# The opening of a diffusion backbone step: first modulation's weights in ring buffers, six units ahead on the first half of h, idle matmuls on TensorE

## The chip, the cores and the metric

The kernel runs on one core of one Trainium2 chip. The metric is the time of one execution on the device in microseconds (us). Before the change it is 2283.66 us, the median of 3 runs (2283.55 to 2283.94).

## What is computed

One inference step of a two-layer backbone on 512 latent tokens and 128 context tokens of width 1024, all in float32. Each layer is a half-step SwiGLU FFN, a token mixer (a Fourier mixer in layer 0, attention in layer 1) and another half-step FFN. Each sub-layer stands in a norm whose shift, scale and gate come from the conditioning vectors. Only the opening of layer 0 matters here:

```python
def _modulation(cond, w_mod, b_mod):
    m = jax.nn.silu(cond) @ w_mod + b_mod
    return m.reshape(cond.shape[0], N_MOD, D_MODEL)

def _modulated_prenorm(x, g, m, k):
    return _rmsnorm(x, g) * (1 + m[:, 3 * k + 1, None]) + m[:, 3 * k, None]

def _half_ffn(x, m, k, g_pre, g_post, w1, w2):
    h = _modulated_prenorm(x, g_pre, m, k)
    return x + 0.5 * m[:, 3 * k + 2, None] * _rmsnorm(_swiglu(h, w1, w2), g_post)
```

So the first FFN can't multiply by `w1` before the first two of the nine modulation vectors (shift and scale) are there, each a product of the conditions with 1024 x 1024 weights.

## The kernel before

Activations lie transposed: 8 chunks of 128 channels on the partitions, the 640 tokens as columns in two halves of 320. A float32 product is made of three fast ones: each operand is split into a rounded part `hi` (ScalarE, L215) and the rest `lo` (VectorE, L216), and `mm3` (L228 to L230) multiplies hi x hi, hi x lo and lo x hi. In the profile's names of a product, `main<-ring,hi`, the first input is h and the second the weights.

A *unit* is one 128 x 1024 block of weights: a 512 KB load into one of 4 `raw` buffers (L157) and a split into a `hi` and a `lo` buffer (6 of each, the pool `wts`), or, for a few units, into two blocks of the ring of 20 (`ring`, 128 x 1280). Units 0 and 1 are gate and up of the FFN's column 0, units 2 and 3 of column 1, 4 and 5 of column 2, 6 and 7 (in ring blocks) of column 3. One unit times one half of h is 8 chunks x 3 = 24 products.

`begin` (L299) opens the kernel:

- x of the first half is loaded. `first` (L383) squares and sums it, TensorE adds over the channels (L502), GpSimd takes the power (L507), TensorE spreads the result over the partitions (L512), and VectorE scales x into `y` (L391).
- The weights of shift and scale come as 16 loads of 512 KB (`first`, L320) in two parts of 8. Part 0 gives the coefficients of chunks 0 to 3, part 1 those of chunks 4 to 7. They take `hi` and `lo` buffers of the pool of units. Each tile is multiplied by four small matmuls (128x256, 32 rows of output, L323) as it lands.
- `coefs` (L333): ScalarE reads the sums (L330), TensorE turns them (L346), and VectorE makes the coefficients in four small operations (L339, L434 to L438). Then the four chunks get scale and shift, by VectorE for even (L400) and by ScalarE for odd ones (L398), and are split.
- `products` (L353) multiplies chunks 0 to 3 by units 0 and 1, then comes part 1 of the weights, then chunks 0 to 3 by units 2 and 3. What is left, chunks 4 to 7 of these four units, is kept in `begun` and run by `ffn` (L602) as its first step. Units 4 to 7 and the other half of h follow there. The norm of the other half (`launch`, `pre`) is woven between, with its L502 and L512 on TensorE and its L538, L544 and L546 on VectorE and ScalarE.

All loads but two of x go through SyncE's queue in the order of the program. Every engine works through its own list in order; a scheduler settles that order when the program is built, with marked stretches (`high_priority`) ahead and `behind_of` holding an instruction behind others. So a row that waits holds all rows after it on its engine.

Of the kernel before, what the change touches and what calls it, by code (L numbers as in the profile page):

```python
# [18 lines left out]
P = 128  # L19
# [91 lines left out]
class Kernel:  # L111
    def __init__(self, ctx, tc, io, subs=6):
        self.tc, self.nc, self.io, self.subs = tc, tc.nc, io, subs
        pool = lambda name, bufs, **k: ctx.enter_context(tc.tile_pool(name=name, bufs=bufs, **k))
        self.keep = pool("keep", 1)
        self.raw = pool("raw", NRAW)
        self.wts = pool("wts", NWU)
        self.blkp = pool("blk", NBLK)
        self.dram = pool("dram", 1, space=bass.MemoryType.DRAM)
        self.tmp = pool("tmp", 1)  # L120
        self.small = pool("small", 8)
        self.psum = pool("psum", 8, space=PSUM)
        self.serial = 0
        self.background = []
        self.units = []
        self.loaded = {}
        self.split_done = {}
        self.sent = 0
        self.now = 0.0
        self.side = [None, None]  # L130
        self.normed = [[True, True], [True, True]]
        self.woven = []
        self.latest = None
        self.xs = {}
        self.hs = {n: Hidden(self.ring, n % 3 != 1) for n in range(DEPTH * 3)}
        self.fast, self.mixed = {}, []
# [18 lines left out]
    def raw_tile(self, src, width=UNIT):  # L155
        t = self.raw.tile([P, UNIT], F32, tag="raw", name=self.name("raw"))[:, :width]
        self.nc.sync.dma_start(out=t, in_=src)  # L157
        return t
# [116 lines left out]
    def setup(self):  # L275
# [17 lines left out]
        nc.sync.dma_start(out=self.sk, in_=io["conds"])  # L293
# [3 lines left out]
        nc.sync.dma_start(out=self.vec, in_=io["vec"])  # L297

    def begin(self):  # L299
# [12 lines left out]
        room = lambda: [self.wts.tile([P, UNIT], F32, tag=("hi", "lo")[k % 2], name=self.name("first")) for k in range(NCH)]  # L312

        def weights(part, tiles, steps=(), units=()):
            out = ps[:, part * 256 : (part + 1) * 256]
            for k, raw in enumerate(tiles):
                if k in units:
                    with self.behind_of(self.load):
                        ws.append(self.unit(len(ws), 0))
                self.load = nc.sync.dma_start(out=raw, in_=io["w_mod_k"][part, k])  # L320
                with self.behind_of(*[self.latest] if part else []):
# [4 lines left out]
                if k in steps:  # L326
                    next(chain)
            rows = self.temp("left")[:, :256]
# [31 lines left out]
        rows = weights(0, room(), (1, 3, 5))  # L360
        later = room()
        with self.behind_of(self.load):
            ws = [self.unit(0, 0)]
        coefs(0, rows)
        with self.behind_of(self.load, *self.entered):
            ws.append(self.unit(1, 0))
        pss = [self.bank() for _ in range(2)]
        for j in range(2):
            products(pss[j:], ws[j : j + 1], range(4))
        rows = weights(1, later, units=(5, 6))  # L370
        with self.behind_of(self.load):
            for c in range(0, NCH, 2):
                nc.sync.dma_start(out=self.xpair(0, c, 1), in_=io["x"][:, c : c + 2, HALF:])
            self.load = nc.sync.dma_start(out=self.wide, in_=io["cond_rows"].unsqueeze(0).to_broadcast([P, 2, D]))
        pss += [self.bank() for _ in range(2)]
        products(pss[2:], ws[2:], range(1))
        coefs(1, rows)
        products(pss[2:], ws[2:], range(1, 4))
        self.begun = [partial(products, pss[i : i + 2], ws[i : i + 2], range(4, NCH)) for i in (0, 2)], pss
# [222 lines left out]
    def ffn(self, layer, which, base, boundary):  # L602
# [12 lines left out]
        def w1(fs, half):  # L615
# [4 lines left out]
            if n == half == 0 and 0 in fs:  # L620
                rest, pss = self.begun
# [809 lines left out]
```

## Time and profile before

| | us |
|---|---|
| median of 3 runs | 2283.66 |
| profiled execution, first to last instruction (span) | 2280.3 |
| difference, before the first and after the last instruction | 3.4 |
| TensorE busy with matmuls | 2250.1 (99%) |
| VectorE busy | 1732.2 (76%) |
| ScalarE busy | 1269.6 (56%) |
| TensorE waiting for the loads of the first modulation | 12.1 |

The page gives the profiled execution by its span alone. A row of the timeline has its start, its length, engine, line and operation, what is written and read, a count, and in brackets the idle time before it with what ended it. PE is TensorE, PEld its weight loads, DVE VectorE, ACT ScalarE, POOL GpSimd and SP SyncE; PEclk is the granted share of TensorE's full clock. A matmul row lasts until its modelled end; the next is issued earlier, so the rate is read from the starts.

### The profile page before, as it was taken

The numbers are of one execution on the slowest core, as the hardware profiler recorded it, in microseconds if no ns is written. First come the engines' busy times: TensorE is split into PE (matmuls) and PEld (weight loads), VectorE is DVE, ScalarE is ACT, GpSimd is POOL, SyncE is SP. The second block draws the span as 40 slices with busy tenths as digits, with TensorE's granted clock in tenths as the row PEclk, the third lists the DMA queues.
The fourth block names the chain that finished last, engine by engine and source line by source line (L and its number), as shares of the span: only waits on it lengthen the run. The fifth ranks groups of instructions, "written<-read, shape, count | busy, mean of one in ns | idle before, by whom it ended". The sixth has DMA issues, their size and how long they took to land.

```text
span 2280.3 us, 39327 instructions
## 1 busy us (share of the span) xinstructions
PE 2250.1 (99%) x15680; PEld 2211.6 (97%) x15680; DVE 1732.2 (76%) x3014; ACT 1269.6 (56%) x2460; POOL 43.1 (2%) x64
## 2 busy tenths in 40 slices
PE   7999999999999999999999999999999999999998
PEld 5999999999999999999999999998998999999998
DVE  5889888588788888868878888587667485766674
ACT  4445554565654555556545544567778654545545
POOL 0000000000000000000000000000000000000000
PEclk9999999999999999999999999999999999999999
DMA  8244543434333433443234443324333223322322
GB/s 313 88 138 150 162 133 113 147 97 129 112 112 112 148 121 125 135 157 112 92 123 145 151 130 110 140 92 140 112 108 116 67 74 101 111 93 76 104 92 100
DMA packets 80281, 278.14 MB, mean 122 GB/s; under 512 B 8800, under 2 KB 15200, under 8 KB 79968
## 3 DMA queue, kind: packets, MB, share of 16 engines
q1 hardware_dynamic: 79280, 274.63, 36.4%
q8 instruction: 123, 2.02, 0.3%
q10 hardware_dynamic: 816, 0.98, 0.1%
q14 instruction: 62, 0.51, 0.1%
HBM read 264.04 MB, written 11.53 MB: 121 GB/s over the span
## 4 chain that ended last, share of the span: by engine, by line
PE 95%; DVE 2%; DMA 1%; ACT 1%; issue 0%; DVEq 0%; POOL 0%; SPq 0%
PE main L228 28%; PE main L230 27%; PE main L229 27%; PE score L229 3%; PE score L228 3%; PE score L230 3%; PE sum L1262 1%; PE score L1219 1%; PE sum L512 1%; PE sum L502 1%; DMA first<-in_w_mod_k 1%; PE turn L1246 1%; DVE lo L216 0%; PE main L1246 0%; DVE ring L1065 0%
## 5 line engine op out<-in xcount | busy, mean ns | idle before, releaser
L228 PE MATMUL main<-ring,hi 128*128 128x320 f32 x3872 | 1206.5, 312 | 2.0 <-ACT ring L215 1.6
L229 PE MATMUL main<-ring,hi 128*128 128x320 f32 x3872 | 1198.2, 310 | 1.0 <-DVE ring L216 1.0
L230 PE MATMUL main<-ring,lo 128*128 128x320 f32 x3872 | 1198.4, 310 | 0.0
L228 PEld LDWEIGHTS main<-ring,hi 128*128 128x128 f32 x3872 | 728.0, 188 | 8.4 <-issue 4.1
L229 PEld LDWEIGHTS main<-ring,hi 128*128 128x128 f32 x3872 | 728.3, 188 | 2.1 <-DVE ring L216 1.6
L230 PEld LDWEIGHTS main<-ring,lo 128*128 128x128 f32 x3872 | 728.0, 188 | 0.6 <-issue 0.5
L215 ACT ACTIVATE hi<-raw 128x1024 fp32r<-128x1024 f32 (+1 forms) x366 | 356.0, 974 | 433.7 <-PE main L229 349.2
L216 DVE TENSOR_TENSOR lo<-raw,hi 128x1024 fp32r<-128x1024 f32 (+1 forms) x366 | 409.0, 1118 | 140.8 <-ACT hi L215 139.4
L421 DVE SCALAR_TENSOR_TENSOR junk<-raw,wide 128x1024 bf16<-128x1024 f32 x256 | 312.7, 1222 | 19.7 <-DMA raw<-in_w_mod_t 17.2
L763 ACT ACTIVATE y<-main 128x320 f32<-128x320 f32 x318 | 135.7, 432 | 150.1 <-PE main L230 149.4
L737 ACT ACTIVATE main<-y 128x320 f32<-128x320 f32 x256 | 111.4, 439 | 39.2 <-DVE left L719 27.0
L228 PE MATMUL score<-ring,hi 128*128 128x320 f32 x416 | 128.9, 310 | 0.0
L230 PE MATMUL score<-ring,lo 128*128 128x320 f32 x416 | 128.6, 309 | 0.0
L229 PE MATMUL score<-ring,hi 128*128 128x320 f32 x416 | 128.5, 309 | 0.0
L216 DVE TENSOR_TENSOR lo<-sums,hi 128x1024 fp32r<-128x1024 f32 x72 | 88.0, 1222 | 42.6 <-ACT hi L215 42.6
L457 DVE TENSOR_TENSOR total<-total,square 128x640 f32<-128x640 f32 x71 | 58.4, 824 | 79.9 <-ACT square L456 78.2
L215 ACT ACTIVATE hi<-sums 128x1024 fp32r<-128x1024 f32 x72 | 76.3, 1060 | 33.8 <-DVE sums L181 19.6
L228 PE MATMUL main<-ring,ring 128*128 128x320 f32 x288 | 90.9, 316 | 0.0
L230 PE MATMUL main<-ring,ring 128*128 128x320 f32 x288 | 89.1, 310 | 0.0
L229 PE MATMUL main<-ring,ring 128*128 128x320 f32 x288 | 88.9, 309 | 0.0
L228 PEld LDWEIGHTS score<-ring,hi 128*128 128x128 f32 x416 | 78.1, 188 | 0.0
L229 PEld LDWEIGHTS score<-ring,hi 128*128 128x128 f32 x416 | 78.1, 188 | 0.0
(195 smaller groups left out, 2604.8 us busy)
## 6 DMA issues: line engine op xcount, KB each, us to landing
raw<-in_w SPq DMA_DIRECT2D x264, 512.0 KB, 3.6
raw<-in_w_mod_t SPq DMA_DIRECT2D x128, 512.0 KB, 4.1
raw<-in_qkv SPq DMA_DIRECT2D x26, 512.0 KB, 3.7
first<-in_w_mod_k SPq DMA_DIRECT2D x16, 512.0 KB, 8.9
spill<-ring SPq DMA_DIRECT2D x12, 640.0 KB, 3.8
ring<-spill SPq DMA_DIRECT2D x12, 640.0 KB, 7.0
raw<-in_bias SPq DMA_DIRECT2D x16, 448.0 KB, 3.4
raw<-in_four_in SPq DMA_DIRECT2D x8, 512.0 KB, 5.7
```

Of the source, the lines that this page charges most:

```text
L215: a = self.nc.scalar.activation(hi, src, AF.Copy)
L216: return a, self.nc.vector.tensor_tensor(lo, src, hi.bitcast(F32), op=ALU.subtract)
L228: mm(out, whi, xhi, start=start, stop=False)
L229: mm(out, whi, xlo, start=False, stop=False)
L230: self.latest = mm(out, wlo, xhi, start=False, stop=stop)
L421: last = self.nc.vector.scalar_tensor_tensor(out=self.junk, in0=raw, scalar=1.0, in1=self.wide[:, cond, :], op0=ALU.mult, op1=ALU.mult, ac ...
L457: nc.vector.tensor_tensor(acc, acc, sq, op=ALU.add)
L502: self.meant = nc.tensor.matmul(ps[:, j : j + 1], part[:, t : t + P], self.mean, start=i == j == 0 or len(acc) == 1, stop=i == len(acc) - ...
L512: self.spread = nc.tensor.matmul(bank[:, t : t + P], col[:, j : j + 1].to_broadcast([P, P]), self.ident, start=True, stop=True)
L737: nc.scalar.activation(ps[:, :HALF], self.y[:, m, lo:hi], AF.Copy)
L763: nc.scalar.activation(self.y[:, m, lo:hi], ps[:, :HALF], AF.Copy)
L1219: nc.tensor.matmul(o, q, k[:, BLOCK_KEYS[b]], start=part == 0, stop=part == 1)
```

## The change

- The 16 weight tiles lie in ring blocks, not in the pool of units (`fetch`). All of part 0 is asked for first, then units 0 and 1, then part 1 with units 2 and 3 between its tiles, then units 4 and 5, then x of the other half.
- `begin` multiplies chunks 0 to 3 by four units ahead of part 1 and by units 4 and 5 behind it, in two banks of the kind `score`. `ffn` then runs chunks 4 to 7 of units 0 to 3 and, as a second step, of 4 and 5.
- `warm` puts pairs of 128x128 matmuls of ones, whose result nobody reads, ahead of tiles 4 to 7 of part 0 and one pair ahead of the first products.
- The conditions' load goes to ScalarE's queue, and that of `vec` behind the fourth tile of part 0.

```diff
--- before.py
+++ after.py
@@ -130,7 +130,8 @@
         self.side = [None, None]
         self.normed = [[True, True], [True, True]]
         self.woven = []
-        self.latest = None
+        self.latest = self.load = None
+        self.entered = ()
         self.xs = {}
         self.hs = {n: Hidden(self.ring, n % 3 != 1) for n in range(DEPTH * 3)}
         self.fast, self.mixed = {}, []
@@ -154,7 +155,7 @@
 
     def raw_tile(self, src, width=UNIT):
         t = self.raw.tile([P, UNIT], F32, tag="raw", name=self.name("raw"))[:, :width]
-        self.nc.sync.dma_start(out=t, in_=src)
+        self.fetched = self.nc.sync.dma_start(out=t, in_=src)
         return t
 
     def unit(self, i, ahead=3):
@@ -290,11 +291,10 @@
         nc.vector.memset(self.power, -0.5)
         nc.vector.memset(self.mod, 0.0)
         make_identity(nc, self.ident)
-        nc.sync.dma_start(out=self.sk, in_=io["conds"])
+        nc.scalar.dma_start(out=self.sk, in_=io["conds"])
         self.conds = self.temp("right")[:, : NCH * 32].rearrange("p (k m) -> p k m", m=32)
         nc.vector.memset(self.conds, 0.0)
         nc.scalar.activation(self.conds[:, :, :2], self.sk, AF.Silu)
-        nc.sync.dma_start(out=self.vec, in_=io["vec"])
 
     def begin(self):
 
@@ -309,22 +309,37 @@
         next(chain)
         ps = self.bank("turn")
         sel = self.ident.rearrange("p (j r) -> p j r", j=4)[:, :, :2]
-        room = lambda: [self.wts.tile([P, UNIT], F32, tag=("hi", "lo")[k % 2], name=self.name("first")) for k in range(NCH)]
-
-        def weights(part, tiles, steps=(), units=()):
+        idle = self.bank()
+        ws, arrived = [], {}
+
+        def fetch(part, k):
+            raw = arrived[part, k] = self.ring(F32)[:, :UNIT]
+            with self.behind_of(*[self.load] if self.load else []):
+                self.load = nc.sync.dma_start(out=raw, in_=io["w_mod_k"][part, k])
+
+        def unit():
+            with self.behind_of(self.load, *self.entered):
+                ws.append(self.unit(len(ws), 0))
+            self.load = self.fetched
+
+        def warm(n):
+            for _ in range(n):
+                with self.behind_of(self.latest):
+                    self.latest = nc.tensor.matmul(idle[:, :P], self.ones, self.ones, start=True, stop=True)
+
+        def weights(part, steps=()):
             out = ps[:, part * 256 : (part + 1) * 256]
-            for k, raw in enumerate(tiles):
-                if k in units:
-                    with self.behind_of(self.load):
-                        ws.append(self.unit(len(ws), 0))
-                self.load = nc.sync.dma_start(out=raw, in_=io["w_mod_k"][part, k])
-                with self.behind_of(*[self.latest] if part else []):
+            for k in range(NCH):
+                raw = arrived.pop((part, k))
+                with self.behind_of(*[self.latest] if self.latest else []):
                     for j in range(4):
                         last = nc.tensor.matmul(out[32 * j : 32 * j + 32], self.conds[:, k, :],
                                                 raw[:, j * 256 : (j + 1) * 256], start=k == 0, stop=k == NCH - 1)
                 self.latest = last
                 if k in steps:
                     next(chain)
+                if part == 0 and 2 < k < NCH - 1:
+                    warm(2)
             rows = self.temp("left")[:, :256]
             with self.tc.high_priority():
                 nc.scalar.activation(rows, out, AF.Copy)
@@ -357,26 +372,35 @@
                         self.mm3(p[:, :HALF], w[0][:, k * P : (k + 1) * P], w[1][:, k * P : (k + 1) * P], *h.chunk(k, 0),
                                  k == 0, k == NCH - 1)
 
-        rows = weights(0, room(), (1, 3, 5))
-        later = room()
-        with self.behind_of(self.load):
-            ws = [self.unit(0, 0)]
+        for k in range(NCH):
+            fetch(0, k)
+            if k == 3:
+                with self.behind_of(self.load):
+                    self.load = nc.sync.dma_start(out=self.vec, in_=io["vec"])
+        rows = weights(0, (1, 3, 5))
         coefs(0, rows)
-        with self.behind_of(self.load, *self.entered):
-            ws.append(self.unit(1, 0))
-        pss = [self.bank() for _ in range(2)]
-        for j in range(2):
+        warm(2)
+        unit()
+        unit()
+        for k in range(NCH):
+            fetch(1, k)
+            if k in (1, 3):
+                unit()
+        pss = [self.bank() for _ in range(4)]
+        for j in range(4):
             products(pss[j:], ws[j : j + 1], range(4))
-        rows = weights(1, later, units=(5, 6))
+        rows = weights(1)
+        pss += [self.bank("score") for _ in range(2)]
+        for j in (4, 5):
+            unit()
         with self.behind_of(self.load):
             for c in range(0, NCH, 2):
-                nc.sync.dma_start(out=self.xpair(0, c, 1), in_=io["x"][:, c : c + 2, HALF:])
+                self.load = nc.sync.dma_start(out=self.xpair(0, c, 1), in_=io["x"][:, c : c + 2, HALF:])
             self.load = nc.sync.dma_start(out=self.wide, in_=io["cond_rows"].unsqueeze(0).to_broadcast([P, 2, D]))
-        pss += [self.bank() for _ in range(2)]
-        products(pss[2:], ws[2:], range(1))
         coefs(1, rows)
-        products(pss[2:], ws[2:], range(1, 4))
-        self.begun = [partial(products, pss[i : i + 2], ws[i : i + 2], range(4, NCH)) for i in (0, 2)], pss
+        products(pss[4:], ws[4:], range(4))
+        self.begun = {fs: ([partial(products, pss[i : i + 2], ws[i : i + 2], range(4, NCH)) for i in at], pss[at[0] : at[-1] + 2])
+                      for fs, at in (((0, 1), (0, 2)), ((2,), (4,)))}
         self.later = [partial(nc.scalar.activation, self.wide, self.wide, AF.Silu)]
         self.launch(1, self.pre(0, 0, 1, fold=4500), 3000)
 
@@ -617,8 +641,8 @@
                 if f not in g:
                     g[f] = self.ring(F32R).rearrange("p (a t) -> p a t", a=2)
             pss = []
-            if n == half == 0 and 0 in fs:
-                rest, pss = self.begun
+            if n == half == 0 and fs in self.begun:
+                rest, pss = self.begun[fs]
                 for go in rest:
                     go()
             elif len(fs) == 1:
```

ScalarE's order at the first split of units, before. `left` is its read of the modulation's sums, `ring` the hi of a chunk of h, `hi` that of a unit; unit 0 is `hi_200`.

```order
L330 ACTIVATE left_188<-turn_122 128x256
L215 ACTIVATE hi_200<-raw_198 128x1024
L215 ACTIVATE ring_212<-y 128x320
L398 ACTIVATE y<-y,coef 128x320
L215 ACTIVATE ring_212<-y 128x320 x2
L398 ACTIVATE y<-y,coef 128x320
L215 ACTIVATE ring_212<-y 128x320
L215 ACTIVATE hi_231<-raw_229 128x1024
```

And with the change, where unit 0 is `hi_228`:

```order
L345 ACTIVATE left_197<-turn_121 128x256
L422 ACTIVATE y<-y,coef 128x320
L216 ACTIVATE ring_207<-y 128x320 x3
L422 ACTIVATE y<-y,coef 128x320
L216 ACTIVATE ring_207<-y 128x320
L216 ACTIVATE hi_228<-raw_226 128x1024
L216 ACTIVATE hi_234<-raw_232 128x1024
L216 ACTIVATE hi_244<-raw_242 128x1024
L216 ACTIVATE hi_254<-raw_252 128x1024
```

The first unit's split has moved from ahead of the four chunks' rows to behind them, where now all four units stand. ScalarE's order around its read of part 1's sums, before (`hi_288` and `hi_299` are units 2 and 3):

```order
L215 ACTIVATE hi_288<-raw_286 128x1024
L215 ACTIVATE hi_299<-raw_297 128x1024
L330 ACTIVATE left_313<-turn_122 128x256
L398 ACTIVATE y<-y,coef 128x320
L215 ACTIVATE ring_336<-y 128x320 x3
L398 ACTIVATE y<-y,coef 128x320
L215 ACTIVATE ring_336<-y 128x320
```

And with the change (`hi_356` and `hi_362` are units 4 and 5):

```order
L216 ACTIVATE hi_254<-raw_252 128x1024
L345 ACTIVATE left_350<-turn_121 128x256
L216 ACTIVATE hi_356<-raw_354 128x1024
L422 ACTIVATE y<-y,coef 128x320
L216 ACTIVATE ring_379<-y 128x320 x3
L422 ACTIVATE y<-y,coef 128x320
L216 ACTIVATE hi_362<-raw_360 128x1024
L216 ACTIVATE ring_379<-y 128x320
```

Two units' splits stood ahead of that read and two chunks' scalings; now unit 4 stands behind the read and unit 5 behind the chunks' rows. VectorE's order around the norm of the other half, before. `ring_462` and `ring_468` are the lo of units 6 and 7, L538 scales x by the norm, and `right` is the FFN's product of gate and up:

```order
L216 TENSOR_TENSOR ring_462<-raw_459,ring_461 128x1024
L216 TENSOR_TENSOR ring_468<-raw_465,ring_467 128x1024
L538 TENSOR_TENSOR y<-ring_102,rms_501 128x2x320
L538 TENSOR_TENSOR y<-ring_103,rms_501 128x2x320
L544 TENSOR_SCALAR y<-y,coef 128x192
```

And with the change, where `ring_543` is the lo of unit 6:

```order
L562 TENSOR_TENSOR y<-ring_101,rms_525 128x2x320
L662 TENSOR_TENSOR right_534<-score_353,left_533 128x320
L568 TENSOR_SCALAR y<-y,coef 128x192
L568 TENSOR_SCALAR y<-y,coef 128x128
L562 TENSOR_TENSOR y<-ring_102,rms_525 128x2x320
L217 TENSOR_TENSOR ring_495<-right_534,ring_495 128x320
L568 TENSOR_SCALAR y<-y,coef 128x192
L217 TENSOR_TENSOR ring_543<-raw_540,ring_542 128x1024
L568 TENSOR_SCALAR y<-y,coef 128x128
L217 TENSOR_TENSOR ring_549<-raw_546,ring_548 128x1024
L217 TENSOR_TENSOR ring_578<-y,ring_577 128x640
```

The lo's of units 6 and 7 stood ahead of the norm's first row and now stand seven and nine rows behind it.

On TensorE, chunks 0 to 3 of units 0 to 3 now stand ahead of part 1 of the weights (L336), and behind it, between the turn of its sums (L361) and the first product on chunk 4, those of units 4 and 5.

## The prediction

> **What bounds the kernel now.** I read the page first, then the busy time by stretches of the start, the waits of TensorE there, and the timeline of each engine up to 60 us. The page shows a kernel that is TensorE's from end to end:
>
> ```profile
> span 2280.3 us, 39327 instructions
> PE 2250.1 (99%) x15680; PEld 2211.6 (97%) x15680; DVE 1732.2 (76%) x3014; ACT 1269.6 (56%) x2460; POOL 43.1 (2%) x64
> ```
>
> What it loses, it loses at the start (columns: PE, PEld, DVE, ACT, POOL busy, granted clock, DMA share, GB/s):
>
> ```profile
> 20.00:30.00 10.00, 7.62 (x60) 6.17 (x64) 5.59 (x15) 4.68 (x9) 0.00 (x0) 0.83 0.96 381
> 30.00:40.00 10.00, 7.11 (x48) 4.50 (x40) 3.66 (x8) 2.48 (x5) 0.00 (x0) 0.68 0.95 346
> 40.00:50.00 10.00, 10.00 (x70) 9.99 (x69) 7.34 (x16) 9.28 (x15) 0.00 (x0) 0.98 0.53 211
> ...
> 23.00:24.00 1.00, 0.95 (x5) 0.65 (x5) 0.85 (x3) 0.97 (x3) 0.00 (x0) 0.63 1.03 414
> ...
> 26.00:27.00 1.00, 1.00 (x7) 1.00 (x6) 0.00 (x0) 0.00 (x0) 0.00 (x0) 0.66 1.04 414
> ...
> 30.00:31.00 1.00, 0.92 (x17) 0.16 (x8) 0.61 (x1) 0.35 (x1) 0.00 (x0) 1.00 0.46 70
> ...
> 33.00:34.00 1.00, 0.43 (x5) 0.20 (x8) 1.00 (x1) 0.00 (x0) 0.00 (x0) 0.75 0.97 384
> ...
> 40.00:41.00 1.00, 1.00 (x7) 1.00 (x7) 0.76 (x3) 1.00 (x4) 0.00 (x0) 0.83 0.99 401
> ```
>
> The first wait is the largest, and the clock halves twice: from about 23.3 to 26.7 and from 33.5 to 40.3, that is one and two stretches of 3.4 us. From 40.3 on TensorE neither waits nor runs slow up to 100 us.
>
> ```profile
> PE turn L323 <- DMA first<-in_w_mod_k: 12.1, 4, 9.1
> ```
>
> A product (one matmul of 128x320) is issued each 0.147 us at full clock: these two rows are three products apart, 0.44.
>
> ```profile
> 27.10 0.31 PE L228 MATMUL main<-ring,hi 128*128 128x320 f32 x1
> ...
> 27.54 0.31 PE L228 MATMUL main<-ring,hi 128*128 128x320 f32 x1
> ```
>
> So a stretch of 3.4 us at half clock costs 3.4/2 = 1.7 us. Each engine's instructions stand in the same order as before behind the first 75 us or so, so the change is worth what TensorE gains or loses by then. I follow it to a common mark: the first product of the unit after the first six (unit 6).
>
> **Step 1, first half of the modulation.** Removed ahead of it: two transfers on SyncE's queue. Moved: x stands first there, 0.92 us earlier (0.73, where the queue began, against 1.65).
>
> ```profile
> 0.73 0.39 SPq L293 DMA_DIRECT2D sk<-in_conds  x1
> ...
> 1.65 0.94 SPq L307 DMA_DIRECT2D ring<-in_x  x2
> ...
> 14.52 1.65 PE L512 MATMUL sum<-ident,col 128*128 128x128 f32 x6
> 16.10 1.64 PE L323 MATMUL turn<-first,right 128*32 128x256 f32 x24
> 17.95 0.64 PE L323 MATMUL turn<-first,right 128*32 128x256 f32 x8 [0.21 <-DMA first<-in_w_mod_k]
> 18.66 0.38 ACT L330 ACTIVATE left<-turn 128x256 f32<-128x256 f32 x1 [2.01 <-PE turn L323]
> 19.09 0.61 PE L346 MATMUL sum<-ident,left 128*128 128x8 f32 x4 [0.50 <-ACT left L330]
> ...
> 20.34 0.80 DVE L400 TENSOR_SCALAR y<-y,coef 128x320 f32<-128x320 f32 x2
> ```
>
> The norm's transposes (L512) then end near 15.2 in place of 16.1. Behind them stood four tiles of 1.64/3 = 0.55 us; now an idle pair goes ahead of each. No idle matmul is in the trace. A pair is four of L512's instructions: 4/6 of 0.83 us at full clock (row in step 5), 0.55, or of 1.65, 1.1. I take 0.55, as the clock was full from 16.1 on: 15.2 + 4 x (0.55 + 0.55) = 19.6 us, against 17.95 + 0.64 = 18.59: the filler costs 1.0 us, as the tiles no longer catch up after L512. Bounds: 17.7 (all hidden, transfers 0.9 us earlier) and 21.8 (all at 1.1). Call this end G. The conditions' load, now ahead of ScalarE's two x loads, costs that queue one issue (0.4 us) and x hides it. vec lands long before its use at G.
>
> **Step 2, the splits of units 0 to 3.** Before, the first unit's split ran while VectorE made the coefficients; now all four stand behind the splits of chunks 0 to 3.
>
> ```profile
> 19.22 1.06 ACT L215 ACTIVATE hi<-raw 128x1024 fp32r<-128x1024 f32 x1 [0.18 <-DMA raw<-in_w]
> ...
> 20.82 0.47 ACT L215 ACTIVATE ring<-y 128x320 fp32r<-128x320 f32 x1 [0.54 <-DVE y L400]
> 21.06 1.22 DVE L216 TENSOR_TENSOR lo<-raw,hi 128x1024 fp32r<-128x1024 f32 x1
> 21.20 0.64 ACT L398 ACTIVATE y<-y,coef 128x320 f32<-128x320 f32 x1
> 21.34 0.41 PE L228 MATMUL main<-ring,hi 128*128 128x320 f32 x1 [1.64 <-ACT ring L215]
> ...
> 22.19 1.29 DVE L216 TENSOR_TENSOR ring<-y,ring 128x320 fp32r<-128x320 f32 x3
> ...
> 22.73 0.42 PE L229 MATMUL main<-ring,hi 128*128 128x320 f32 x1 [0.98 <-DVE ring L216]
> ...
> 23.51 1.04 ACT L215 ACTIVATE hi<-raw 128x1024 fp32r<-128x1024 f32 x1
> ```
>
> The coefficients end 20.34 - 18.59 = 1.75 after G; ScalarE's six chunk rows take 23.51 - 20.82 = 2.7; then hi 1.06 and lo 1.22. TensorE's third product comes at G + 6.75 = 26.35; before, its second came at 22.73. Later lo's follow each 1.2 us and hide behind 12 products (1.76).
>
> The clock: TensorE idles some 4 us here with one idle pair and two products in it. Before, a gap from 19.70 to 22.73 with one product cost one stretch, so I charge 1.7. The 46 products left: 26.35 + 46 x 0.147 + 1.7 = 34.8.
>
> **Step 3, second half.** Ring buffers remove the wait for slots; the dip to 70 GB/s at 30 goes, and the last weights land about 1.4 us earlier, near 33.7. Nobody waits for that any more:
>
> ```profile
> 28.07 3.09 PE L323 MATMUL turn<-first,right 128*32 128x256 f32 x48
> ...
> 35.05 1.08 PE L323 MATMUL turn<-first,right 128*32 128x256 f32 x8 [0.40 <-DMA first<-in_w_mod_k]
> ...
> 40.28 0.34 PE L228 MATMUL main<-ring,hi 128*128 128x320 f32 x1
> ```
>
> Six tiles took 3.09, eight take 4.1: E = 38.9, with 48 products done. Before it was 36.1 with 24.
>
> **Step 4, units 4 and 5.** Their splits are queued on ScalarE behind its read of the second half, hence behind E, and TensorE's chunks 4 to 7 behind their products. After E on ScalarE: read 0.38, hi of unit 4 1.06. Coefficients at E + 1.75; y 0.80, lo of unit 4 1.22, three chunk lo's 1.29: E + 5.1. Beside it ScalarE's y, three chunk rows and y (the 2.7 of step 2 less one chunk row), 2.3, and hi of unit 5 1.06: also E + 5.1. Lo of unit 5: E + 6.35. So 53 products are done at 38.9 + 6.4 = 45.3. Before, 36 were done at 40.28, hence 53 at 42.8: the change is 2.5 us behind, and has idled 5 us, which I charge 1.5 of the 1.7 at half clock. x of the other half now waits for two units' 1 MB on SyncE's queue, 2.6 us at the 401 GB/s of the row at 40, but it is first read behind all this, after E + 5.
>
> **Step 5, unit 6.** Its split was ahead of the second half's norm; now it is behind it on both engines.
>
> ```profile
> 52.37 2.36 DVE L216 TENSOR_TENSOR ring<-raw,ring 128x1024 fp32r<-128x1024 f32 x2
> ...
> 52.42 0.83 PE L512 MATMUL sum<-ident,col 128*128 128x128 f32 x6
> ...
> 53.29 0.44 ACT L518 ACTIVATE rms<-sum 128x320 f32<-128x320 f32 x1
> 54.65 1.55 DVE L538 TENSOR_TENSOR y<-ring,rms 128x640 f32<-128x640 f32 x2
> 55.50 1.37 ACT L546 ACTIVATE y<-y,coef 128x192 f32<-128x192 f32 x3 [0.90 <-DVE y L538]
> 56.12 1.18 DVE L544 TENSOR_SCALAR y<-y,coef 128x192 f32<-128x192 f32 x4
> ...
> 57.49 0.31 PE L228 MATMUL main<-ring,ring 128*128 128x320 f32 x1
> 57.81 0.48 DVE L638 TENSOR_TENSOR right<-score,left 128x320 f32<-128x320 f32 x1
> ```
>
> From the end T of L512: ScalarE's rms 0.48; VectorE's y 0.78, product 0.45, two y 0.59, y 0.78, chunk lo 0.45, y 0.30, lo of unit 6 half of 2.36, 1.18: T + 5.0. TensorE has six products left at T (0.88, some of it under L512's tail) and wants unit 6 at T + 0.8; two products pass on hi, so it stands 3.9 us. Before, unit 6 was whole at 52.37 + 1.18, 3.9 us ahead of 57.49. The gap lowers the clock again, three times in four: 1.2. Later work keeps its slack: chunks 0 to 3 of the second half are due 7 us after unit 6 begins (48 products), and VectorE has some 4 us of work up to them.
>
> **Sum.** 2.5 + 1.5 + 3.9 + 1.2 = 9.1 us later at the mark (the 1.0 of step 1 and the 1.7 of step 2 are in the 2.5). The span is 2280.3; the median of the three runs, 2283.66, has 3.4 us around it, which stay. Forecast: 2292.8 us.
>
> **A rule.** The clock's rows say that gaps broken by some products do lower it. [...]
>
> **Rivals.**
> - *The clock stays.* The pairs and stray products keep it full in all three gaps: 9.1 - 1.7 - 1.5 - 1.2 = 4.7, 2288.4. For: no gap is wholly empty. Against: the half clock at 23.3. 0.14.
> - *Unit 6 isn't late* (its split finds room as before): 9.1 - 3.9 - 1.2 = 4.0, 2287.7. Against: both engines' rows. 0.07.
> - *Transfers alone hold TensorE.* If the splits kept pace and TensorE only waited for weights, E = 33.7 + 0.6 with 48 done, units 4 and 5 follow at once: 72 done at 34.3 + 0.6 + 3.5 = 38.4, against 40.28 + 36 x 0.147 = 45.6: faster by 7.2, 2276.5. It decides if the first products run by 23.5 and unit 4 is split by E. For: the DMA share near 1. Against: steps 2 and 4. 0.06.
> - *Longer half clock*, two stretches each, as from 33.5 to 40.3: 3 or 4 us more, 2296. 0.07.
>
> **Numbers.** The forecast has 0.66, with 2289.5 to 2295.5 from G's bounds and the clock. A measurement here tells 0.2%, 4.6 us, from no change. Slower takes the forecast, the long clock and half of the first rival (4.7 against 4.6): 0.80; same the second rival and the other half: 0.14; faster 0.06. The range, 2286.9 to 2295.9, takes in the first two rivals and leaves out the fast one and the tails.
>
> **What would show it.** Right: hi of the first unit starting near 24 and the first products near 25 to 26; the last second-half tile landing before TensorE reads it; units 4 and 5 split after E, with some 5 us of TensorE idle; 4 us idle ahead of unit 6; clock 0.5 near 27, 44 and 64. Wrong: TensorE waiting on weights near 33, or full clock throughout, or unit 6 starting without a wait.

## The result and the profile after

The changed kernel takes 2294.25 us (median of 4 runs, 2293.79 to 2295.7) where the kernel before, run beside it, takes 2283.61 (2282.82 to 2283.94): a ratio of 1.0053, 95% interval 1.0041 to 1.0064. It is slower, by 10.6 us by the medians. The profiled execution took 2294.42 us, of which the span is 2292.6; before, the span was 2280.3.

The page's row of busy times of the changed kernel:

```profile
PE 2255.9 (98%) x15700; PEld 2216.8 (97%) x15700; DVE 1732.3 (76%) x3014; ACT 1269.5 (55%) x2460; POOL 44.0 (2%) x64
```

TensorE has 20 rows more (the ten idle matmuls), and the share of its time that is busy is smaller. The same stretches as before, and the stalls that now stand in three of them, at 20, 40 and 60 us:

```profile
20.00:30.00 10.00, 5.28 (x38) 3.55 (x37) 6.32 (x18) 6.46 (x11) 0.00 (x0) 0.75 1.03 409
30.00:40.00 10.00, 10.00 (x99) 8.69 (x101) 2.29 (x3) 0.46 (x1) 0.00 (x0) 0.91 1.05 397
40.00:50.00 10.00, 6.21 (x36) 4.66 (x29) 7.82 (x19) 8.50 (x14) 0.00 (x0) 0.77 0.67 234
...
60.00:70.00 10.00, 6.53 (x43) 6.00 (x43) 6.71 (x14) 6.50 (x12) 1.06 (x1) 0.97 0.01 2
```

Between 30 and 40 the transfers run at 397 GB/s where they had 346, and TensorE never waits for them there. The waits of TensorE up to 100 us (total, times, longest) name what it waits for in place of them:

```profile
PE turn L336 <- DMA ring<-in_w_mod_k: 8.2, 2, 7.5
PE main L229 <- ACT hi L216: 3.9, 1, 3.9
PE main L229 <- ACT ring L216: 2.8, 1, 2.8
PE score L231 <- DVE lo L217: 2.1, 2, 1.7
...
PE score L229 <- ACT hi L216: 1.2, 2, 0.9
...
PE main L231 <- DVE ring L217: 0.7, 1, 0.7
PE main L231 <- DVE lo L217: 0.4, 1, 0.4
```

The wait for the first modulation's loads fell from 12.1 to 8.2 us, 3.9 less; 11.1 us of waits for splits stand there where 2.6 us stood before (1.6 and 1.0), and not one of them is for a transfer. The marks of the prediction on TensorE: first and third product, part 1's tiles, third product of unit 5, third product of unit 6.

```profile
27.67 0.64 PE L229 MATMUL main<-ring,hi 128*128 128x320 f32 x1 [3.86 <-ACT hi L216]
...
28.93 0.64 PE L231 MATMUL main<-ring,lo 128*128 128x320 f32 x1 [0.36 <-DVE lo L217]
...
37.15 3.66 PE L336 MATMUL turn<-ring,right 128*32 128x256 f32 x64
...
47.09 0.64 PE L231 MATMUL score<-ring,lo 128*128 128x320 f32 x1 [0.36 <-DVE lo L217]
...
68.40 0.41 PE L231 MATMUL main<-ring,ring 128*128 128x320 f32 x1 [0.70 <-DVE ring L217]
```

Before, that last product stood at 57.78: 10.6 us later at the mark. The rest of the 12.3 us of span is clock: here are the stretches of 3.4 us around its three drops (columns as in the stretches above; the second is PE's busy time, the third from the end the clock).

```profile
21.59:25.00 3.41, 1.72 (x16) 1.04 (x16) 1.39 (x7) 1.49 (x4) 0.00 (x0) 0.99 1.03 408
25.00:28.39 3.39, 0.72 (x2) 0.50 (x2) 2.89 (x9) 3.36 (x6) 0.00 (x0) 0.50 1.03 408
28.39:31.78 3.39, 3.03 (x12) 2.85 (x12) 3.39 (x4) 2.07 (x3) 0.00 (x0) 0.50 1.03 411
42.03:45.44 3.41, 0.97 (x3) 0.48 (x3) 3.34 (x10) 3.06 (x7) 0.00 (x0) 1.00 0.36 142
45.44:48.85 3.41, 2.66 (x8) 2.26 (x9) 3.29 (x8) 3.15 (x6) 0.00 (x0) 0.50 0.72 193
62.52:65.93 3.41, 1.85 (x15) 1.58 (x13) 1.94 (x5) 1.95 (x5) 0.00 (x0) 1.00 0.00 0
65.93:69.34 3.41, 1.50 (x8) 1.24 (x9) 3.41 (x6) 3.41 (x6) 0.00 (x0) 1.00 0.00 0
69.34:72.74 3.40, 3.40 (x15) 3.40 (x14) 3.40 (x6) 0.78 (x2) 0.00 (x0) 0.50 0.51 158
```

Each of the three drops follows a stretch in which TensorE was busy for about half of it or less (1.72, 0.97, 1.50 of 3.4). In this trace the half clock ended behind stretches that were nearly full (3.03, 3.40); behind 2.66 of 3.4 it stayed for another stretch, up to 52.3. The busy time alone doesn't foretell a drop: the stretch up to 65.93 had 1.85 and kept the full clock, while in the run with four units below one with 2.44 (51.58 to 55.00) lost it. The changes of the clock (25.0, 31.8, 45.4, 52.3, 69.3, 72.7) lie whole multiples of 3.41 us apart, to 0.1 us. So do those in the kernel before (23.3, 26.7, 33.5, 40.3), and in the runs below with ring blocks alone (24.05, 34.3, 41.1) and with the first gap filled (46.0, 52.8, 66.5, 73.3); from trace to trace they stand at other places. The third drop, at 69.34, lies behind the mark and costs 3.4/2 = 1.7: 10.6 + 1.7 = 12.3.

### The profile page after: what moved, and what is told of

It is laid out like the page before. It is cut to its first block, busy times and chain, and to the rows that moved or that the text cites. A ratio compares the mean times of both kernels' runs of the same rounds, so it can differ in the third digit from the quotient of the medians.

```text
span 2292.6 us, 39364 instructions
## 1 busy us (share of the span) xinstructions
PE 2255.9 (98%) x15700; PEld 2216.8 (97%) x15700; DVE 1732.3 (76%) x3014; ACT 1269.5 (55%) x2460; POOL 44.0 (2%) x64
## 4 chain that ended last, share of the span: by engine, by line
PE 94%; DVE 2%; ACT 1%; DMA 1%; issue 1%; DVEq 0%; POOL 0%; ACTq 0%
PE main L229 27%; PE main L231 27%; PE main L230 27%; PE score L231 3%; PE score L230 3%; PE score L229 3%; PE sum L1286 1%; PE score L1243 1%; PE sum L536 1%; PE sum L526 1%; DVE lo L217 1%; PE turn L1270 1%; PE main L1270 0%; DMA ring<-in_x 0%; PE turn L336 0%
## 5 line engine op out<-in xcount | busy, mean ns | idle before, releaser
L231 PEld LDWEIGHTS score<-ring,lo 128*128 128x128 f32 x416 | 79.0, 190 | 2.8 <-DVE lo L217 2.8
L229 PEld LDWEIGHTS score<-ring,hi 128*128 128x128 f32 x416 | 79.0, 190 | 1.5 <-ACT hi L216 1.5
```

The lines of the kernel that those rows point to most:

```text
L229: mm(out, whi, xhi, start=start, stop=False)
L231: self.latest = mm(out, wlo, xhi, start=False, stop=stop)
```

## The experiments

Theory: three changes of order each have a price of their own (the first unit's split behind the chunks of h, those of units 4 and 5 behind the read of part 1's sums, that of unit 6 behind the norm of the other half), and the idle matmuls cost time and hold no clock. Rivals: the stalls are bound by something else (transfers, six units as such), or are one loss that appears at another place when one is removed. Times are medians; 2294.25 is what each is held against unless the text says the kernel before (2282.5 to 2283.2 in these comparisons). The changed kernel was not run again beside them, and the kernel before was 0.4 to 1.1 us faster there than beside it (2283.61), so each gain on 2294.25 may be that much too large. A trace is one execution, and one stretch of half clock more or less is up to 1.7 us.

### No idle matmuls

```diff
-                if part == 0 and 2 < k < NCH - 1:
-                    warm(2)
...
-        warm(2)
```

> The changed kernel without its ten idle matmuls, all else alike. Theory (the fillers stand in the way): four pairs of about 0.65 us and a first one of 1.0 stand between the norm's transposes and the last tile of part 0, so its read moves from 22.2 to about 19.3 us and all behind it with it: 2.5 to 3 us faster than the change, 2291.5. Rival (the fillers keep the clock): without them TensorE halves its clock earlier and gives the 3 us back: 2294 to 2296.

Measured: 2291.27 (2290.75 to 2293.24), ratio to before 1.0037 (1.0023 to 1.0051). The theory's side, 3.0 us back (2.1 by the distance to the kernel before). The rival, that the gain is given back, falls, although the gap that they leave is longer:

```profile
24.19 0.64 PE L229 MATMUL main<-ring,hi 128*128 128x320 f32 x1 [4.84 <-ACT hi L216]
...
34.30 3.66 PE L336 MATMUL turn<-ring,right 128*32 128x256 f32 x64
```

The first product comes 3.48 us sooner, and part 1's tiles 2.85. Three drops of the clock stand in this trace too, and the third lasts two stretches (63.8 to 70.7), not one.

### The first unit asked for ahead of the coefficients

```diff
+        unit()
         coefs(0, rows)
         warm(2)
         unit()
-        unit()
```

> The changed kernel with the first unit asked for ahead of the coefficients, as before the change, so that its split stands ahead of the chunks' rows on ScalarE. Theory (the splits' order holds TensorE): third product of the first unit at the read of part 0 plus 4 us in place of 6.8, the end of part 1's weights as much earlier: 2.5 us faster than the change, 2291.7. Rival (TensorE is held by part 1's weights): it waits for them instead, no gain: 2294.

Measured: 2291.98 (2290.57 to 2292.57), ratio 1.0039 (1.0024 to 1.0054): 2.3 us back, as the theory had it. The wait of 3.9 us for the first unit's hi is gone; the first product stands at 24.62 and part 1's tiles at 35.17, 2.0 us sooner.

### Units 4 and 5 split ahead of the read of part 1's sums

```diff
-        rows = weights(1)
-        pss += [self.bank("score") for _ in range(2)]
         for j in (4, 5):
             unit()
+        rows = weights(1)
+        pss += [self.bank("score") for _ in range(2)]
...
-            with self.tc.high_priority():
+            with self.tc.high_priority(), self.behind_of(*[self.cut] if part else []):
                 nc.scalar.activation(rows, out, AF.Copy)
```

(`self.cut` is the hi of the split that the program wrote last.)

> The changed kernel with the splits of units 4 and 5 put ahead of ScalarE's read of part 1's sums. Theory: the 3.3 us of waits at their products (42.3 to 47.1) go, and the half clock that they bring, 6.8 us long from 45, goes or shortens: 5 to 7 us faster than the change, 2288. Rival: the wait moves to the first product on chunk 4, whose rows are queued behind the two more splits: 1 to 2 us, 2292.5.

Measured: 2288.69 (2286.95 to 2289.49), ratio 1.0026 (1.0016 to 1.0035): 5.6 us back. Both waits of the products of units 4 and 5 are gone, and with them the clock's second drop; the wait for unit 6 stays:

```profile
40.00:50.00 10.00, 9.50 (x71) 9.13 (x64) 6.11 (x18) 8.19 (x14) 0.00 (x0) 1.00 0.59 234
50.00:60.00 10.00, 7.22 (x52) 6.96 (x51) 5.67 (x14) 4.30 (x9) 1.06 (x1) 1.00 0.00 0
```

The profiled execution took 2286.95, the fastest of the ten and 1.7 below their median. So a usual one may have a stretch of half clock more; no trace shows one.

### Units 6 and 7 sent ahead of the norm of the other half

```diff
+        with self.behind_of(self.load):
+            self.unit(5, 2)
         self.later = [partial(nc.scalar.activation, self.wide, self.wide, AF.Silu)]
```

> The changed kernel with the loads and splits of units 6 and 7 written ahead of the first step of the FFN, so that they stand ahead of the other half's norm. Theory: the waits of 2.8 and 0.7 us at unit 6 go, and the half clock behind them (1.7): 3.5 to 5.2 us faster than the change, 2289 to 2291. Rival: VectorE and ScalarE only change which is late, and TensorE waits for the other half's chunks: under 1 us, 2293.5.

Measured: 2289.15 (2288.46 to 2290.21), ratio 1.0028 (1.0017 to 1.0038): 5.1 us back. From 60 to 70 us TensorE neither waits nor runs slow, the rest is as in the changed kernel:

```profile
60.00:70.00 10.00, 10.00 (x73) 10.00 (x73) 7.88 (x17) 5.99 (x14) 1.23 (x1) 1.00 0.12 46
```

### Four units ahead

```diff
-        pss += [self.bank("score") for _ in range(2)]
-        for j in (4, 5):
-            unit()
...
-        products(pss[4:], ws[4:], range(4))
```

(`begun` keeps its first entry alone.)

> The changed kernel with four units ahead in place of six: units 4 and 5 are asked for and split where ffn comes to them, chunks 4 to 7 of units 0 to 3 follow part 1. My theory (the stalls behind the end of part 1's weights and ahead of unit 6 come from the places of units 4 to 7 in the orders): the idle 5 us behind part 1 shrink to the 2.5 or so that the coefficients need, and unit 4's split comes in time as before: 6 to 8 us below the changed kernel, 2286 to 2288. Rival (six units do what they are for, cover the second half's coefficients): without them TensorE idles there for longer, 2294 to 2297.

Measured: 2287.46 (2284.84 to 2289.84), ratio 1.0019 (1.001 to 1.0028): 6.8 us back, inside the theory's range. Behind part 1 TensorE now waits 1.7 us for the coefficients and later 1.0 for unit 4's split, and unit 6 is in time. So units 4 and 5, in the places that the change gave them, cost more than they cover.

### The loads in the order of before

```diff
-        nc.scalar.dma_start(out=self.sk, in_=io["conds"])
+        nc.sync.dma_start(out=self.sk, in_=io["conds"])
...
+        nc.sync.dma_start(out=self.vec, in_=io["vec"])
...
-            if k == 3:
-                with self.behind_of(self.load):
-                    self.load = nc.sync.dma_start(out=self.vec, in_=io["vec"])
```

> The changed kernel with one part undone: the conditions' load and that of vec stand on SyncE's queue ahead of x, as before. My theory: the last of x lands about 0.9 us earlier, the transposes of the norm end near 14.5 us in place of 15.3, and as the four tiles behind them are held by matmuls and idle pairs the end of part 0 moves by the same 0.7 to 1.0 us: 2293.3. Rival (what I put into the prediction: x is first on the queue and gains by it): the end of part 0 comes 0.7 to 0.9 us later, 2295.1.

Measured: 2292.79 (2292.36 to 2293.53), ratio 1.0046 (1.0029 to 1.0063): 1.5 us below the changed kernel, the theory's side, but 0.4 by the distance to the kernel before, so the times don't show it. The trace does: the last tile of part 0 starts at 20.47 in place of 21.51. What moved is the two x loads that go through ScalarE's queue. Their row among the DMA issues (KB each, median us from issue to landing), in the changed kernel:

```profile
ring<-in_x ACTq DMA_DIRECT2D x2, 320.0 KB, 6.3
```

and with the order of before:

```profile
ring<-in_x ACTq DMA_DIRECT2D x2, 320.0 KB, 3.6
```

The edit takes the conditions' load from in front of these two and also starts the weight tiles on SyncE's queue later, as two loads stand ahead there again. Which of the two does it, no run separates.

### All four mended

No idle matmuls, the first unit early, units 4 to 7 as in the runs above; the loads stay as in the change.

> Four edits at once: no idle matmuls, unit 0 asked for ahead of the coefficients, units 4 and 5 split ahead of the read of part 1's sums, units 6 and 7 sent ahead of the norm of the other half. Alone they measured 3.0, 2.3, 5.6 and 5.1 us below the changed kernel's 2294.25, 16 together. My theory (each of the orders has its own price on a different stretch of the chain, and the prices nearly add): 2278 if they add wholly, 2279 to 2282 allowing that units 4 and 5 land only near 35 to 36 us and so hold TensorE a little; below the kernel before by 1 to 5 us. Rival (the gains overlap: a stall that goes is taken up by the next one, and the clock drops all the same): 2284 to 2287, no better than the kernel before.

Measured: 2279.57 (2278.93 to 2283.23), ratio to before 0.9991 (0.9981 to 1.0): 14.7 us below the changed kernel, of the 16 that the four gave alone. The rival (one loss that moves) falls. Against the kernel before it is 2.9 us less by the medians, with an interval that ends at 1.0, so hardly clear of no difference; at the mark of the prediction (third product of unit 6) it stands at 55.22 against 57.78. What bounds it behind part 1 is the transfers of units 4 and 5, which their hi's wait for. ScalarE's rows there are the hi's of units 4 and 5 and the read:

```profile
35.35 1.06 ACT L216 ACTIVATE hi<-raw 128x1024 fp32r<-128x1024 f32 x1 [6.59 <-DMA raw<-in_w]
36.64 1.06 ACT L216 ACTIVATE hi<-raw 128x1024 fp32r<-128x1024 f32 x1 [0.23 <-DMA raw<-in_w]
37.60 0.37 ACT L343 ACTIVATE left<-turn 128x256 f32<-128x256 f32 x1
```

### All four mended, loads in the order of before

> The four edits of the run above, and besides the loads in the order of before: the conditions and vec on SyncE's queue ahead of x. My theory: with them on ScalarE's queue the conditions and the last of x landed later, and the norm's transposes ended 0.7 us later than before; so here they end 0.7 to 1.0 us earlier than in the run above, and the time is 0.5 to 1 us less than there, 2278 to 2281. Rival (the queue's order is worth what stands ahead on it, 0.9 us): x lands 0.9 us later and the time is 0.5 to 1 us more.

Measured: 2280.72 (2279.02 to 2282.81), ratio 0.9993 (0.9983 to 1.0002). A miss: no gain on the run above. Part 0 does end earlier, and part 1's tiles start 1.6 us sooner (32.02 against 33.62), but units 4 and 5 land when they did (their hi's start at 35.27 and 36.62, against 35.35 and 36.64):

```profile
32.02 3.66 PE L337 MATMUL turn<-ring,right 128*32 128x256 f32 x64
38.00 1.02 PE L360 MATMUL sum<-ident,left 128*128 128x8 f32 x4 [2.32 <-ACT left L344]
```

TensorE waits 2.3 us for the read in place of 0.7, and in this execution, the slowest of its ten, the clock fell behind it (0.76 from 40 to 50 us, where it was 1.00 in the run above).

### Unit 4 asked for ahead of the last two tiles of part 1

The edit is made to the run above.

```diff
-            if k in (1, 3):
+            if k in (1, 3, 5):
                 unit()
...
-        for j in (4, 5):
-            unit()
         rows = weights(1)
+        unit()
```

(Part 1's first scaling on ScalarE is held behind unit 5's hi.)

> The run with four edits and the loads in the order of before, and one thing more: unit 4 is asked for ahead of the last two tiles of part 1, unit 5 behind them, so the read of part 1's sums stands behind unit 4's split alone. In the two runs without this, unit 4 landed at 35.3 us and unit 5 at 36.6, and the read of the sums, which could have run at 35.7 or at 37.3, ran at 37.6. My theory (what is left there is the order of the transfers): unit 4 lands near 33, the last tile near 35.3, the read runs at 36, the products of unit 4 start near 36.5 in place of 38.5 to 38.9, unit 5 costs 1 us of waiting at most: 1 to 2.5 us below the four edits' 2279.6, that is 2277 to 2278.5. Rival (a wait for the last tile near 33 to 35 takes the place of the wait for the read, and the clock falls there): 2279.5 to 2281.

Measured: 2279.91 (2278.38 to 2284.02), ratio 0.9991 (0.9982 to 1.0): the rival's number, though not by its mechanism. Unit 3 now lands later (TensorE waits 0.8 and 0.7 us for its split), the last tile is no wait at all, and the lo of unit 5 stands behind the coefficients' rows on VectorE:

```profile
40.54 0.64 PE L231 MATMUL score<-ring,lo 128*128 128x320 f32 x1 [1.74 <-DVE lo L217]
```

The three mended versions can't be told apart by their medians.

### The kernel before with ring blocks alone

```diff
-        room = lambda: [self.wts.tile([P, UNIT], F32, tag=("hi", "lo")[k % 2], name=self.name("first")) for k in range(NCH)]
+        room = lambda: [self.ring(F32)[:, :UNIT] for k in range(NCH)]
```

> The kernel before with one part of the change alone: the 16 tiles of the first modulation lie in ring blocks, in the same order of loads. My theory: the dip of the transfers to 70 GB/s at 30 us (a load waiting for its buffer) goes, the last tile of part 1 lands some 1.4 us earlier, and as TensorE waits for it there, the time falls by 1 to 2 us, to 2280.5 to 2281.5. Rival (the work behind it waits for the coefficients or the splits anyway): no change, 2282.5.

Measured: 2282.59 (2280.53 to 2283.69), ratio 0.9998 (0.9989 to 1.0007): no change, my theory fell. The last tile does come earlier, and the next product with it (before at 35.05 and 36.06, 1.3 us later):

```profile
33.99 0.84 PE L323 MATMUL turn<-ring,right 128*32 128x256 f32 x8 [0.65 <-DMA ring<-in_w_mod_k]
34.76 0.64 PE L228 MATMUL main<-ring,hi 128*128 128x320 f32 x1
...
41.11 0.32 PE L230 MATMUL main<-ring,lo 128*128 128x320 f32 x1
...
49.85 0.41 PE L230 MATMUL score<-ring,lo 128*128 128x320 f32 x1 [0.64 <-DVE lo L216]
```

But the clock's second drop now lies later. Its edges with ring blocks:

```profile
34.00:34.50 0.50, 0.50 (x8) 0.14 (x8) 0.00 (x0) 0.00 (x0) 0.00 (x0) 0.79 1.06 358
41.00:41.50 0.50, 0.50 (x5) 0.50 (x4) 0.47 (x3) 0.50 (x2) 0.00 (x0) 0.88 1.00 401
```

and in the kernel before:

```profile
33.50:34.00 0.50, 0.43 (x5) 0.20 (x8) 0.50 (x1) 0.00 (x0) 0.00 (x0) 0.51 0.88 350
40.00:40.50 0.50, 0.50 (x4) 0.50 (x4) 0.26 (x2) 0.50 (x2) 0.00 (x0) 0.67 0.99 401
```

It lasts 6.8 us in both, but from 34.3 to 41.1 with ring blocks and from 33.5 to 40.3 before. So 20 products run at half clock, where 12 did: of the 1.3 us 0.35 are left behind it (the 21st product from there on stands at 41.11, before at 40.28 + 8 x 0.147 = 41.46). The first drop stands 0.8 us later as well (24.05 for 23.26), though the first products ahead of it start within 0.1 us of before's. So the 0.8 doesn't come from the rows ahead; what it does come from, and whether the medians are equal for this reason, is not shown. The wait of 0.64 us at 49.85 takes what is left: unit 4's split now stands behind the activation of `wide`, 1.9 us, on ScalarE.

### The kernel before with the idle matmuls alone

```diff
...
+                if part == 0 and 2 < k < NCH - 1:
+                    warm(2)
...
         coefs(0, rows)
+        warm(2)
```

> The kernel before with the ten idle matmuls alone (four pairs ahead of tiles 4 to 7 of part 0, a pair ahead of the first products). My theory: each pair costs TensorE 0.6 us, the end of part 0 comes 1.5 to 2.5 us later, the clock falls all the same at about 25: 2284 to 2285. Rival (they hold the clock over the gap): the half clock from 23.3 to 26.7 goes, 1.7 us back: 2282 to 2283.

Measured: 2285.76 (2284.41 to 2287.09), ratio 1.0012 (1.0003 to 1.0021): 3.2 us more, the theory's side and a little beyond it. The last tile of part 0 starts at 20.63 in place of 17.95, and the clock falls all the same, in this trace for two stretches (23.8 to 30.7) where the kernel before had one; so not all of the 3.2 us need be the filler's own time. The stretch ahead of that drop:

```profile
20.50:23.90 3.40, 1.92 (x18) 1.13 (x17) 1.41 (x7) 1.73 (x4) 0.00 (x0) 0.99 1.03 410
```

### The first gap filled

```diff
         coefs(0, rows)
-        warm(2)
+        warm(13)
```

> The changed kernel with thirteen idle matmuls in place of two behind the turn of the first sums, so that they cover the whole wait for the first unit's split (23.1 to 27.7 us; two of them took 0.57 to 0.69 us, thirteen take about 3.9). The eight ahead of tiles 4 to 7 stay. My theory (the clock falls because a stretch of 3.4 us is mostly idle, and two matmuls are too few to alter that): TensorE stays at full clock through the first products, which then take 0.147 us each from 27.7 on, the half clock at 25.0 to 31.8 goes, and of its cost 2.0 us come back: 2292.0 to 2292.5. Rival (idle matmuls don't hold the clock however many): they run at half speed themselves, 13 take 7 us, the first products come near 30.5, and the time is 2 to 4 us more, 2296 to 2298.

Measured: 2297.05 (2293.49 to 2298.95), ratio to before 1.0057 (1.0043 to 1.0071), 2.8 us above the changed kernel by the medians, though the two ratios' intervals overlap. The clock in the first gap is the theory's, the time is the rival's. In this execution there is no drop in that gap (the clock is 1.00 from 20 to 40 us): 13 matmuls (x26 rows) fill 3.15 us, and the first products run at full rate.

```profile
23.97 3.15 PE L328 MATMUL main<-ones 128*128 128x128 f32 x26
28.54 0.42 PE L229 MATMUL main<-ring,hi 128*128 128x320 f32 x1 [1.42 <-ACT hi L216]
...
36.74 3.66 PE L336 MATMUL turn<-ring,right 128*32 128x256 f32 x64
```

The stretches in which the changed kernel's three drops lie:

```profile
26.00:28.00 2.00, 1.12 (x11) 0.93 (x9) 1.52 (x5) 1.97 (x5) 0.00 (x0) 1.00 1.02 410
...
46.00:48.00 2.00, 1.31 (x5) 1.31 (x6) 2.00 (x7) 1.74 (x4) 0.00 (x0) 0.50 0.85 225
...
66.00:68.00 2.00, 0.84 (x2) 0.50 (x2) 2.00 (x4) 2.00 (x4) 0.00 (x0) 0.61 0.00 0
```

From the first product to part 1's tiles it is 8.2 us where the changed kernel took 9.5, although part 0 ended 0.85 later in this execution. But the gain is gone by unit 6, whose third product stands at 68.42 (68.40 in the changed kernel): the second half clock, from 46.0 to 52.8, ends 0.5 later, and the third starts at 66.5 and lasts two stretches, up to 73.3, in place of one. The span is 4.6 us longer. At 126 us, when the opening is over, TensorE is 0.7 behind the changed kernel, as more of the third half clock lies behind the mark here. Another 2.5 come near 550 us: a wait of 1.0 for a split at 549.19 and a further stretch of half clock from 551.2 to 554.6, neither of which the changed kernel's trace has. The last 1.3 come behind that and are not explained. So most of the loss of this execution lies far behind the opening, and that the filler caused it is not shown.

## Why the prediction was right, step by step

The forecast was 2292.8 in a range of 2286.9 to 2295.9; 2294.25 came. The case was the forecast's own, with the end of part 0 and the clock mis-sized in the sum; a term around the span, too large by luck, hid half of that.

| | predicted | measured |
|---|---|---|
| step 1, end of part 0 (G) | 19.6 | 22.15 |
| step 2, third product | G + 6.75 | G + 6.78 (28.93) |
| step 3, end of part 1 (E) | 38.9 | 40.81 |
| step 4, third product of unit 5 | E + 6.4 | E + 6.28 (47.09) |
| step 4, behind the order of before | 2.5 | 47.09 - 42.8 = 4.3 |
| step 4, half clock behind it | 1.5 | 52.3 - 47.1 at half: 2.6 |
| step 5, wait ahead of unit 6 | 3.9 | 2.77 + 0.70 = 3.5 |
| third half clock | 1.2 | 1.7 |
| sum | 9.1 | 12.1 (span 12.3) |

**Step 1** was mis-sized: G moved by 3.6 us, not 1.0. I moved x 0.9 us earlier, since it is first on SyncE's queue; the last x load landed later instead, and with it the norm.

```profile
0.72 0.45 ACTq L294 DMA_DIRECT2D sk<-in_conds  x1
...
1.21 1.04 ACTq L307 DMA_DIRECT2D ring<-in_x  x2
...
9.84 0.74 ACT L480 ACTIVATE square<-ring 128x640 f32<-128x640 f32 x1 [2.58 <-DMA ring<-in_x]
...
15.25 1.65 PE L536 MATMUL sum<-ident,col 128*128 128x128 f32 x6
16.69 1.06 PE L328 MATMUL main<-ones 128*128 128x128 f32 x4
17.68 0.84 PE L336 MATMUL turn<-ring,right 128*32 128x256 f32 x8
18.45 0.71 PE L328 MATMUL main<-ones 128*128 128x128 f32 x4
```

The transposes start at 15.25 (before 14.52). "x hides it" was the failing clause: with the change, ScalarE's x loads are issued 0.48 us later and take 2.6 us longer to land (6.3 against 3.7 from issue, and 3.6 in the run with the loads' old order). That is 1.5 of the 2.55 us that G was off (the row behind the transposes starts at 16.69, not 15.2). The pairs cost 17.68 - 16.69 = 0.99 for the first and 0.64 for each further one, 2.9 us where I took 4 x 0.55 = 2.2: another 0.7. The tiles between them make up the rest (2.55 for 2.2). The runs without the pairs (3.0 back, or 2.1) and with them alone (3.2 more) agree that about this much is paid at the end, with the clock's part in it not separated.

**Steps 2, 4 and 5** were right in their waits, to 0.4 us each, and each has its own run that takes it away: 2.3, 5.6 and 5.1 us. So the stalls are the orders' and not the transfers', as step 3 had it (the weights of part 1 are waited for no more).

**The clock** was at half rate for 6.8, 6.8 and 3.4 us, against one stretch for each gap. Most of the first 6.8 fell into the wait itself: but for two, products ran in it only from 28.93 to 31.79, at a cost of 1.4 where 1.7 was charged. The second cost 2.6 for 1.5, the third 1.7 for 1.2. So "longer half clock", to which I gave 0.07, came true in two gaps of three, but for 1.3 us in place of its 3 or 4. The larger part of the 3.0 us that the sum was off is step 1's, of which 1.8 is left in step 4's row.

**The ends of the span.** I added 3.4 us for what lies around the span, the median's distance from one execution's span. In the changed kernel's own profiled execution it is 2294.42 - 2292.6 = 1.8, and between 1.7 and 1.9 in every run here. That 1.6 too much hid half of the 3.2 us by which the span's forecast (2289.4) fell short. That is luck: the 2283.66 was held against the span of a faster execution.

**The rivals.** "The clock stays" falls by the drops shown; in the one trace with the first gap filled, 3.15 us of filler stood in it and the clock stayed at 1.00 from 20 to 40 us. "Unit 6 isn't late" falls by the wait of 3.5. "Transfers alone" falls here, but it is what holds the mended versions: there the hi's of units 4 and 5 wait for their landing at 35.35 and 36.64, and neither of the two runs that moved work or loads ahead of that gained anything.

**The rule.** That gaps broken by some products lower the clock held in all three: the drops follow stretches of 3.4 us with 1.72, 0.97 and 1.50 us of busy TensorE, and with the idle matmuls alone one with 1.92. The half clocks lasted 6.8, 6.8 and 3.4 us, one or two stretches each. What sets the places of the changes is not shown: they lie whole multiples of 3.41 us apart, and with ring blocks both drops stand 0.8 us later, though the work ahead of the second moved 1.3 us earlier.

## What to carry to other kernels

More independent work ahead of a stall covered it here only where that work's own preparation stood ahead of the stall on its engine too (5.6 us came back when the splits of units 4 and 5 went ahead of the read): read the order of the engines that prepare it before counting the products. An idle filler delays the matmuls that were about to run behind it (each further pair put 0.64 us between two tiles), and here it bought no time, neither two in a gap (3.0 us back without them) nor thirteen (2.8 us more). A microsecond gained ahead of a half clock can be lost in it, as in the trace with ring blocks, where 0.35 of 1.3 us were left behind it. The first drop stood at 24.05 there and at 23.26 before, behind rows that start within 0.1 us of each other, so a gain of that size is read from many times and not from one trace.

## What the runs showed of the hardware that was not expected

- With a load of 8 KB in front of them on ScalarE's queue, and SyncE's weight tiles issued earlier beside it (from 1.73 us on, 2.63 before), two loads of 320 KB took 6.3 us from issue to landing in place of 3.7 (3.6 with the order of before).
- Half clock followed 3.4 us with as much as 1.92 (the idle matmuls alone) and, once, 2.44 us (four units ahead) of busy TensorE, while 1.85 kept the full clock in the changed kernel: in these traces no share of busy time tells the two apart. In the changed kernel it went on behind 2.66, and full clock came back behind 3.03 and 3.40.
- Within each of four traces (the kernel before, the change, ring blocks alone, the first gap filled) the changes of the clock lay whole multiples of 3.41 us apart; with ring blocks both drops lay 0.8 us later (24.05 for 23.26, 34.3 for 33.5), though the work ahead of the second came 1.3 us earlier. The drop of the first gap was absent with 3.15 us of filler in it, in one trace, at no gain in time (2297.05 for 2294.25).
